# Where one block's 16-bit planes lie at the end of a mixer, and in which order three raw weight tiles are used in the first FFN group

## The chip, the cores and the metric

The kernel runs on one core of a Trainium2 chip. The metric is the device time of one execution in microseconds (us), taken as the median of several runs. TensorE (PE) multiplies matrices, ScalarE (ACT) and VectorE (DVE) work elementwise, GpSimd (POOL) has little to do here, and SyncE (SP) issues nearly all transfers (DMA). Each engine works through its own list of instructions strictly in order and waits for the others on semaphores. SP's list is a queue as well: an instruction that waits on SP holds back every load behind it.

## The reference

A decoder trunk of two layers over 256 tokens of width 2048, all in float32. Each layer adds a mixer and then a SwiGLU FFN to the residual stream `h`; a final RMS norm ends it.

```python
for layer in range(DEPTH):                     # DEPTH = 2
    xn = rms_norm(h, norm_mix[layer])
    if layer % 2 == 0:
        mix = swa_mlstm_mixer(xn, ...)         # ends in  @ w_out   (2048 x 2048)
    else:
        mix = forgetting_attention_mixer(xn, ...)   # ends in  @ w_out
    h = h + mix
    z = rms_norm(h, norm_ffn[layer])
    h = h + (silu(z @ w_gate) * (z @ w_up)) @ w_down    # hidden width 5632
return rms_norm(h, norm_final)
```

The change touches the stretch from the product with `w_out` to the first 512 hidden columns of the FFN (one "group"), once in each layer.

## The kernel before

**Products in three terms.** A float32 product is made of three matmuls of shortened operands: the operand is split into `hi` (a cast on ACT, L206 or L380) and `lo` (the difference on DVE, L207 or L381), and PE adds hi·hi (L557), hi·lo (L558) and lo·hi (L559; L244 to L246 in `gemm`). A load brings a raw chunk of 256 rows by 512 columns of weights (512 KB, L145).

**Mixed pairs.** In a group of the FFN (`pair_group`) gate and up are computed together over eight positions, `ORDER` (L36), each with 256 rows of both matrices. Five positions are plain: two chunks, each split and multiplied. Three, positions 1, 3 and 5, are mixed: the four 128-row blocks (two of gate, two of up) are combined so that seven products do the work of eight. Such a position has a **first stage**, one cast of three blocks (128x1536, L380) with its difference (L381), which fill a slot of `triples` (`hi0`/`lo0` or `hi1`/`lo1`, taken in turn), and a **second stage**, three subtractions in place on DVE (L645, L648, L649) and two more splits of 128x1024. On the other side of each mixed product stand sums of blocks of the activation (`sums_of`, L294 to L297, then a split into `sx`).

**Raw tiles of four blocks.** The raw weights of a mixed position land in a tile of four blocks taken from `quads`, which are used in turn (`quad()`, L113). There are three: two with the tag "quad" in the pool `fp`, and `own`, which lies on the sixth pair of weight planes of the pool `wp` (tag "hi"). The first five pairs are handed to the FFN as `stock`; out_proj's matmuls read the sixth until they end. Before the change `own` stands second in the list, so position 1 takes the first tile, position 3 takes `own`, and position 5 takes the last.

**The end of the mixer.** `out_proj` computes `m @ w_out` in four blocks of 512 columns, n = 0 to 3. `add_out` (L395) adds each to `h`; block n then has to be turned for the FFN, 512 columns at a time. `split_turned` copies it on ACT into two 16-bit planes (`flat`, L338), transposes these by DMA on SP's queue (L340, four transposes a block, into `turned`), and later a `join` on ACT puts the planes together again (two copies, L345) and splits the result into `xh` and `xl` with the gain (L386 on ACT, L387 on DVE). The joins of n = 0 and 1 run within out_proj. Those of n = 2 and 3 are handed on as `todo` and run at positions 3 and 5 of the first FFN group (`LATER`, L53), where the columns are first needed. `scrap(fp, n)` says where `flat` and `turned` lie: for even n in tag "c", for n = 3 in `sd0`/`sd1`, for n = 1 in a tile of tag "quad". The third tile of `quads` therefore has to wait until n = 1 is joined.

**What sets the order.** The program is written per position. The order on each engine is then made by a scheduler that simulates a timeline of the program, so a changed buffer can move instructions on every engine although no line of the loop is edited.

Of the kernel before, what the change touches and what calls it, by code (L numbers as in the profile page):

```python
# [7 lines left out]
F32 = mybir.dt.float32  # L8
BF16 = mybir.dt.bfloat16
F32R = mybir.dt.float32r  # L10
# [7 lines left out]
P = 128  # L18
# [5 lines left out]
NB = 512  # L24
CK = 2
# [29 lines left out]
QUADS = 2  # L55
# [13 lines left out]
def mixed_of(order):  # L69
    return [p for w, p in order if w]  # L70
# [5 lines left out]
def trunk(  # L76
# [27 lines left out]
    stock, triples, quads = [], [], []  # L104

    def slot():
        if not stock:
            both = wp.tile([P, 2, CK, NB], F32R, tag="hi", name="hi")
            return [both[:, a, :, :] for a in range(2)]
        stock.append(stock.pop(0))  # L110
        return stock[-1]
# [255 lines left out]
    def scrap(fp, n):  # L367
        if n % 2 == 0:
            box = fp.tile([P, 4, NB], F32, tag="c", name="box", bufs=1)
            halves = box[:, 0:2, :], box[:, 2:4, :]  # L370
        elif n == 3:
            halves = [fp.tile([P, 3, NB], F32, tag=f"sd{i}", name="box", bufs=1)[:, 0:CK, :] for i in range(2)]
        else:
            box = fp.tile([P, 2 * CK, NB], F32, tag="quad", name="box", bufs=QUADS)
            halves = box[:, 0:2, :], box[:, 2:4, :]
        flat, turned = (a.rearrange("p a n -> p (a n)") for a in halves)
        return flat, turned.bitcast(U16).rearrange("p (b k t q) -> p b k t q", b=2, t=NT, q=P)

# [147 lines left out]
    def spare_halves():  # L526
        return [
            tuple(
                m[:, 8 + 4 * a : 12 + 4 * a, :].rearrange("p k s -> p (k s)").rearrange("p (c n) -> p c n", c=2)
                for m in (mh, ml)  # L530
            )
            for a in range(2)
        ]

    def out_proj(w, idx, key, extra):
        last, rest = KT - 4, []
        for n0 in (0, 2):
            accs = [new_acc() for _ in range(2)]
            for i in range(2):
                gemm(accs[i], m_of, w, (n0 + i) * NB, NB, 0, last, KT, step=6 * i)  # L540
            for i in range(2):
                gemm(accs[i], m_of, w, (n0 + i) * NB, NB, last, KT, KT, step=6)
                add_out(accs[i], n0 + i)
                (later if n0 == 0 else rest).append(
                    (LATER[n0 + i], split_turned(idx, n0 + i, *scrap(extra[3], n0 + i), extra))
                )
                square_sum(key, n0 + i)
        return rest
# [119 lines left out]
    def ffn(layer, fp, sx, x4, sd, key, todo, idx_next=None, key_next=None, finish=None):  # L668
# [8 lines left out]
        for g0, g1 in zip(PARTS, PARTS[1:]):  # L677
# [81 lines left out]
            def close(acc, n):  # L759
                if not end:  # L760
                    add_out(acc, n)
                elif idx_next is None:
                    finish(acc, n, gf)
                else:
                    add_out(acc, n)
                    if n < 1:
                        todo.append((LATER_DOWN[n], split_turned(idx_next, n, *scrap(fp, n))))
                    else:
                        split_scaled(idx_next, n)
                    square_sum(key_next, n)  # L770
# [25 lines left out]
    def close_layer(layer, w_out, idx, key, **rest):  # L796
        with tc.tile_pool(name=f"fp{layer}", bufs=2) as fp:
            junk_of[:] = fp, "tmp", 2
            nx = len(mixed_of(ORDER))
            nd = max(len(mixed_of(o)) for o in DOWN.values())  # L800
            sx = [fp.tile([P, nx, 4, P], F32R, name=f"sx{i}", bufs=1) for i in range(2)]
            x4 = fp.tile([P, 2, P], F32R, name="x4", bufs=1)
            todo = out_proj(w_out, idx, key, (*sx, x4, fp))
            sd = [fp.tile([P, nd, 4, P], F32R, tag=f"sd{i}", name=f"sd{i}", bufs=1) for i in range(2)]
            triples.extend([fp.tile([P, 3, NB], F32R, name=f"{a}{i}", bufs=1) for a in ("hi", "lo")] for i in range(2))
            stock.extend([slot() for _ in range(5)])
            own = wp.tile([P, 2, CK, NB], F32R, tag="hi", name="raw").rearrange("p a k n -> p (a k) n").bitcast(F32)
            quads.extend(fp.tile([P, 2 * CK, NB], F32, tag="quad", name="raw", bufs=QUADS) for _ in range(QUADS))
            quads.insert(1, own)
            ffn(layer, fp, sx, x4, sd, key, todo, **rest)  # L810
            stock.clear()
            triples.clear()
            quads.clear()
# [3 lines left out]
    hi, lo = slot()  # L817
# [17 lines left out]
    with tc.tile_pool(name="ev", bufs=1) as ev:  # L835
# [225 lines left out]
        with tc.tile_pool(name="mp", bufs=1) as mp:  # L1061
# [8 lines left out]
            halves = spare_halves()  # L1070
# [115 lines left out]
    for n in range(4):  # L1186
        nc.gpsimd.dma_start(h[:, :, n * NB : (n + 1) * NB], xv[:, :, n * NB : (n + 1) * NB])

    close_layer(0, w_out_even[0], 2, "f0", idx_next=1, key_next="m1")


    r1 = rstd("m1")
    wi1 = w_in_odd[0]
    with tc.tile_pool(name="od", bufs=1) as od:
# [70 lines left out]
        halves = spare_halves()  # L1265
# [67 lines left out]
    def finish(acc, n, gf):  # L1333
        for t in range(NT):
# [31 lines left out]
            nc.scalar.dma_start(ov[:, t, NB : 2 * NB], b1)  # L1366

    close_layer(1, w_out_odd[0], 3, "f1", finish=finish)


# [47 lines left out]
```

## Time and profile before

| | |
|---|---|
| runs | 2088.95, 2090.94, 2092.37 us; median 2090.94 us |
| profiled execution, its own time | 2090.14 us |
| its span in the trace | 2088.4 us (1.74 us lie around it) |
| busy | PE 2071.4 us (99%), DVE 1806.3 us (86%), ACT 1367.1 us (65%), POOL 44.0 us (2%) |
| in layer 0: end of out_proj, start of the FFN | about 323.3 us from the span's start |
| in layer 1: the same | about 1386 us |

A row of a timeline gives the start of an instruction (or of several alike in a row, "x2"), its duration, engine, line, operation, output and input; in brackets stand the idle time before it on its engine and what ended that. A row of windows gives a stretch of time, for each engine the busy time and the number of instructions, then the granted clock of PE (1.00 is full), the share of the time the DMA engines were busy, and GB/s. PE's matmuls are pipelined: one of 512 columns is listed with some 0.39 us, and starts follow each other every 0.227 us where nothing is missing. So for PE the number of matmuls in a stretch says more than its busy time.

### The profile page before, as it was taken

The page shows a single profiled execution, that of the slowest core. Times are in us where ns is not written, and L with a number is a line of the kernel's source. Part 1 is how long each engine was busy: PE and PEld are TensorE (multiplying, and loading weights), DVE is VectorE, ACT ScalarE, POOL GpSimd, SP SyncE. Part 2 cuts the span into 40 slices and gives each one's busy share as a digit, 9 for nine tenths or more (in the row PEclk, how much of TensorE's full clock was granted, in tenths as well). Part 3 has the DMA queues.
Part 4 walks back from the last instruction along what each step waited for, and adds up shares of the span by engine and source line. Part 5 has one row for each costly group of instructions (what it writes and reads, how often), then busy time and mean ns, then how long its engine had stood idle before and what let it go on. Part 6 is the DMA issues. An engine that isn't in the chain of part 4 may idle for free.

```text
span 2088.4 us, 26470 instructions
## 1 busy us (share of the span) xinstructions
PE 2071.4 (99%) x9473; PEld 1714.7 (82%) x9473; DVE 1806.3 (86%) x2169; ACT 1367.1 (65%) x1649; POOL 44.0 (2%) x69
## 2 busy tenths in 40 slices
PE   9999999999999999999999999999999999999998
PEld 7878887888888888888888888877888888888887
DVE  6788768989999989998899688679989999999984
ACT  6777677665577646667677676587655667556763
POOL 1010000000000000000000001000000000000000
PEclk9999999999999999999999999999999999999999
DMA  8566577765677666665676776585756766666754
GB/s 292 174 207 194 188 242 215 222 200 198 205 221 224 210 194 224 217 209 184 203 202 218 225 200 185 155 269 188 250 188 196 233 196 217 226 205 200 235 158 159
DMA packets 309572, 434.84 MB, mean 208 GB/s; under 512 B 106413, under 2 KB 114625, under 8 KB 309313
## 3 DMA queue, kind: packets, MB, share of 16 engines
q1 hardware_dynamic: 307088, 426.27, 65.1%
q0 software_dynamic: 1632, 5.80, 0.9%
q8 instruction: 74, 1.21, 0.2%
q10 hardware_dynamic: 720, 1.09, 0.2%
q14 instruction: 58, 0.47, 0.1%
HBM read 408.68 MB, written 2.12 MB: 197 GB/s over the span
## 4 chain that ended last, share of the span: by engine, by line
PE 89%; ACT 4%; DVE 3%; DMA 2%; issue 2%; SPq 0%; POOL 0%; POOLq 0%; ACTq 0%; DVEq 0%
PE acc L558 20%; PE acc L559 20%; PE acc L557 20%; PE prod L558 5%; PE prod L557 5%; PE prod L559 5%; PE acc L245 4%; PE acc L244 4%; PE acc L246 4%; DVE hi L207 1%; ACT box L345 1%; PE p L411 1%; ACT hi L206 1%; ACT hi L380 1%; DMA raw<-in_w_gate_dram 1%
## 5 line engine op out<-in xcount | busy, mean ns | idle before, releaser
L206 ACT CAST hi<-raw 128x1024 fp32r<-128x1024 f32 (+3 forms) x561 | 567.1, 1023 | 366.5 <-PE acc L559 179.4
L207 DVE TENSOR_TENSOR hi<-raw,hi 128x1024 fp32r<-128x1024 f32 (+3 forms) x561 | 657.9, 1186 | 137.2 <-ACT hi L206 134.7
L559 PE MATMUL acc<-hi,xl 128*128 128x512 f32 x1320 | 511.9, 389 | 0.0
L557 PE MATMUL acc<-hi,xh 128*128 128x512 f32 x1320 | 495.9, 390 | 0.8 <-ACT xh L386 0.6
L380 ACT CAST hi<-raw 128x1024 fp32r<-128x1024 f32 (+2 forms) x299 | 344.9, 1168 | 225.8 <-PE acc L559 192.7
L558 PE MATMUL acc<-hi,xh 128*128 128x512 f32 x1254 | 488.0, 390 | 0.2 <-DVE hi L207 0.2
L557 PEld LDWEIGHTS acc<-hi,xh 128*128 128x128 f32 x1320 | 247.6, 188 | 53.5 <-ACT xh L386 1.8
L559 PEld LDWEIGHTS acc<-hi,xl 128*128 128x128 f32 x1320 | 248.0, 188 | 51.5
L558 PEld LDWEIGHTS acc<-hi,xh 128*128 128x128 f32 x1254 | 235.4, 188 | 50.0 <-DVE hi L207 1.0
L381 DVE TENSOR_TENSOR hi<-raw,hi 128x1024 fp32r<-128x1024 f32 (+1 forms) x204 | 240.2, 1180 | 11.1 <-ACT hi L380 10.4
L381 DVE TENSOR_TENSOR lo<-raw,hi 128x1536 fp32r<-128x1536 f32 x95 | 166.6, 1754 | 43.6 <-ACT hi L380 40.0
L559 PE MATMUL acc<-hi,ml 128*128 128x512 f32 x466 | 181.0, 389 | 0.0
L557 PE MATMUL acc<-hi,mh 128*128 128x512 f32 x466 | 173.3, 389 | 0.0
L558 PE MATMUL acc<-hi,mh 128*128 128x512 f32 x437 | 170.3, 390 | 0.4 <-DVE hi L207 0.4
L245 PE MATMUL acc<-hi,mh 128*128 128x512 f32 (+1 forms) x322 | 126.3, 392 | 0.0
L244 PE MATMUL acc<-hi,mh 128*128 128x512 f32 (+1 forms) x322 | 125.8, 391 | 0.0
L246 PE MATMUL acc<-hi,ml 128*128 128x512 f32 (+1 forms) x322 | 123.7, 391 | 0.0
L645 DVE TENSOR_TENSOR raw<-raw 128x1024 f32<-128x1024 f32 x95 | 115.5, 1217 | 0.4
L557 PEld LDWEIGHTS acc<-hi,mh 128*128 128x128 f32 x466 | 87.5, 188 | 18.6 <-ACT hi L206 0.4
L559 PEld LDWEIGHTS acc<-hi,ml 128*128 128x128 f32 x466 | 87.5, 188 | 18.1
L245 PE MATMUL acc<-hi,xh 128*128 128x512 f32 (+3 forms) x288 | 99.8, 347 | 0.2 <-DVE hi L207 0.2
L246 PE MATMUL acc<-hi,xl 128*128 128x512 f32 (+3 forms) x288 | 99.1, 345 | 0.0
(364 smaller groups left out, 3073.9 us busy)
## 6 DMA issues: line engine op xcount, KB each, us to landing
raw<-in_w_gate_dram SPq DMA_DIRECT2D x176, 512.0 KB, 4.3
raw<-in_w_up_dram SPq DMA_DIRECT2D x176, 512.0 KB, 4.8
raw<-in_w_down_dram SPq DMA_DIRECT2D x176, 512.0 KB, 4.8
raw<-in_w_in_odd_dram SPq DMA_DIRECT2D x88, 512.0 KB, 5.2
raw<-in_w_in_even_dram SPq DMA_DIRECT2D x51, 512.0 KB, 5.0
raw<-in_w_out_even_dram SPq DMA_DIRECT2D x32, 512.0 KB, 5.3
raw<-in_w_out_odd_dram SPq DMA_DIRECT2D x32, 512.0 KB, 4.7
hr<-in_w_in_even_dram SPq DMA_DIRECT2D x12, 512.0 KB, 4.4
```

Source lines behind the costliest of these rows:

```text
L206: latest[0] = nc.scalar.copy(hi[:, k, 0:n], raw[:, k, 0:n])
L207: nc.vector.tensor_tensor(out=lo[:, k, 0:n], in0=raw[:, k, 0:n], in1=hi[:, k, 0:n].bitcast(F32), op=ALU.subtract)
L244: nc.tensor.matmul(o, ah[:, ts], hi, start=(k == 0), stop=False)
L245: nc.tensor.matmul(o, ah[:, ts], lo, start=False, stop=False)
L246: nc.tensor.matmul(o, al[:, ts], hi, start=False, stop=(k == k_all - 1 and cs.stop == n))
L345: nc.scalar.copy(ju[:, :, b], turned[:, b, :, :, :].rearrange("p k t q -> p (k t q)"))
L380: cast = nc.scalar.copy(dst_h, src)
L381: nc.vector.tensor_tensor(out=dst_l, in0=src, in1=dst_h.bitcast(F32), op=ALU.subtract)
L557: nc.tensor.matmul(o, ah, hi, start=start, stop=False)
L558: nc.tensor.matmul(o, ah, lo, start=False, stop=False)
L559: nc.tensor.matmul(o, al, hi, start=False, stop=stop)
L645: nc.vector.tensor_tensor(out=raw[:, 1:4:2, :], in0=raw[:, 3:4, :].broadcast_to([P, 2, NB]), in1=raw[:, 1:3, :], op=ALU.subtract)
```

## The change

The planes of block n = 1 get another place, the second slot of `triples` (`hi1` for `flat`, `lo1` for `turned`, two of the three blocks of each). The tiles of `triples` carry explicit tags for that. And `own` moves from second to last in the list of `quads`. No line of arithmetic and no size is edited.

```diff
@@ scrap(fp, n): where the planes of h's block n lie
         elif n == 3:
             halves = [fp.tile([P, 3, NB], F32, tag=f"sd{i}", name="box", bufs=1)[:, 0:CK, :] for i in range(2)]
         else:
-            box = fp.tile([P, 2 * CK, NB], F32, tag="quad", name="box", bufs=QUADS)
-            halves = box[:, 0:2, :], box[:, 2:4, :]
+            halves = [fp.tile([P, 3, NB], F32, tag=f"{a}1", name="box", bufs=1)[:, 0:CK, :] for a in ("hi", "lo")]
@@ close_layer
-            triples.extend([fp.tile([P, 3, NB], F32R, name=f"{a}{i}", bufs=1) for a in ("hi", "lo")] for i in range(2))
+            triples.extend([fp.tile([P, 3, NB], F32R, tag=f"{a}{i}", name=f"{a}{i}", bufs=1) for a in ("hi", "lo")] for i in range(2))
             stock.extend([slot() for _ in range(5)])
             own = wp.tile([P, 2, CK, NB], F32R, tag="hi", name="raw").rearrange("p a k n -> p (a k) n").bitcast(F32)
             quads.extend(fp.tile([P, 2 * CK, NB], F32, tag="quad", name="raw", bufs=QUADS) for _ in range(QUADS))
-            quads.insert(1, own)
+            quads.append(own)
```

Behind line 374 the changed kernel's line numbers are one lower (L380 becomes L379). The names carry numbers. Before, the tiles of positions 1, 3 and 5 are raw_2993, raw_2992 (`own`) and raw_2994; in the changed kernel they are raw_2994, raw_2995 and raw_2993 (`own`).

The first place is SP's queue in layer 0's out_proj, around the transposes of n = 0 (box_2579) and n = 1 (box_2647, now box_2647 and box_2648). Before:

```order
L145 DMA raw_2713<-in_w_out_even_dram 128x2x512
L145 DMA raw_2730<-in_w_out_even_dram 128x2x512
L145 DMA raw_2747<-in_w_out_even_dram 128x2x512
L145 DMA raw_2764<-in_w_out_even_dram 128x2x512
L145 DMA raw_2781<-in_w_out_even_dram 128x2x512
L340 DMA_TRANSPOSE box_2579<-box_2579 128x4x128 x4
L340 DMA_TRANSPOSE box_2647<-box_2647 128x4x128 x4
L145 DMA raw_2798<-in_w_out_even_dram 128x2x512
```

Now:

```order
L145 DMA raw_2994<-in_w_gate_dram 128x2x512
L145 DMA raw_2714<-in_w_out_even_dram 128x2x512
L145 DMA raw_2994<-in_w_up_dram 128x2x512
L145 DMA raw_2731<-in_w_out_even_dram 128x2x512
L145 DMA raw_2995<-in_w_gate_dram 128x2x512
L145 DMA raw_2995<-in_w_up_dram 128x2x512
L145 DMA raw_2748<-in_w_out_even_dram 128x2x512
L145 DMA raw_2765<-in_w_out_even_dram 128x2x512
L340 DMA_TRANSPOSE box_2579<-box_2579 128x4x128 x4
L340 DMA_TRANSPOSE box_2648<-box_2647 128x4x128 x4
L145 DMA raw_2782<-in_w_out_even_dram 128x2x512
```

All four loads of positions 1 and 3 have moved ahead of the eight transposes of n = 0 and 1, and one `w_out` load (raw_2781 before, raw_2782 now) has moved behind them.

The second place is the same queue at the start of layer 0's FFN, where the planes of n = 2 (box_2922, now box_2923) and n = 3 (box_2969 and box_2970, now box_2970 and box_2971) are transposed. Before:

```order
L145 DMA raw_2994<-in_w_up_dram 128x2x512
L145 DMA raw_3004<-in_w_gate_dram 128x2x512
L145 DMA raw_3020<-in_w_up_dram 128x2x512
L145 DMA raw_3072<-in_w_gate_dram 128x2x512
L145 DMA raw_3088<-in_w_up_dram 128x2x512
L145 DMA raw_3156<-in_w_gate_dram 128x2x512
L145 DMA raw_3172<-in_w_up_dram 128x2x512
L145 DMA raw_2993<-in_w_gate_dram 128x2x512
L340 DMA_TRANSPOSE box_2922<-box_2922 128x4x128 x4
L145 DMA raw_2992<-in_w_gate_dram 128x2x512
L340 DMA_TRANSPOSE box_2970<-box_2969 128x4x128 x4
L145 DMA raw_2992<-in_w_up_dram 128x2x512
```

Now:

```order
L145 DMA raw_3157<-in_w_gate_dram 128x2x512
L145 DMA raw_3173<-in_w_up_dram 128x2x512
L340 DMA_TRANSPOSE box_2923<-box_2923 128x4x128 x4
L340 DMA_TRANSPOSE box_2971<-box_2970 128x4x128 x4
L145 DMA raw_2993<-in_w_gate_dram 128x2x512
L145 DMA raw_2993<-in_w_up_dram 128x2x512
L145 DMA raw_3243<-in_w_gate_dram 128x2x512
```

The loads of `own` stood between and behind the two groups of transposes and fed position 3; now they stand behind both and feed position 5.

The third place is ACT at the same time. Before:

```order
L206 CAST hi_2987<-raw_3088 128x1024
L380 CAST hi0_2983<-raw_2994 128x1536
L345 COPY box_2969<-box_2970 128x1024 x2
L206 CAST hi_2990<-raw_3156 128x1024
L380 CAST hi1_2985<-raw_2992 128x1536
L345 COPY box_2922<-box_2922 128x1024 x2
L386 ACTIVATE xh_58<-box_2969,gT_93 128x256 x4
L206 CAST hi_2991<-raw_3172 128x1024
L386 ACTIVATE xh_58<-box_2922,gT_93 128x256 x4
```

Now:

```order
L206 CAST hi_2988<-raw_3089 128x1024
L345 COPY box_2923<-box_2923 128x1024 x2
L379 CAST hi_2989<-raw_2995 128x1024
L385 ACTIVATE xh_58<-box_2923,gT_93 128x256 x4
L326 ACTIVATE full_3119<-box_2923,gT_93 128x256 x2
L379 CAST hi_2990<-raw_2995 128x1024
L206 CAST hi_2991<-raw_3157 128x1024
L379 CAST hi0_2984<-raw_2993 128x1536
L345 COPY box_2970<-box_2971 128x1024 x2
L206 CAST hi_2992<-raw_3173 128x1024
```

Before, the cast of position 3's three blocks (into hi1_2985) stood behind the join of n = 3. Now that cast (into hi1_2986) has left this stretch and stands in out_proj, ahead of the last two `w_out` casts; the join of n = 2 comes first, position 3's second-stage casts come next, and the join of n = 3 is behind the three-block cast of position 5. Layer 1 shows the same moves at its mixer's end, with two differences: the four early loads stand there in one run ahead of the last `w_out` load before the eight transposes, and of `own`'s two loads one stands between the transposes of n = 2 and n = 3 and one behind (before, both stood between). On POOL nothing has moved.

## The prediction

> **What bounds the kernel now.** I read the page first: the span, the busy shares and the chain that ended last.
>
> ```profile
> span 2088.4 us, 26470 instructions
> PE 2071.4 (99%) x9473; PEld 1714.7 (82%) x9473; DVE 1806.3 (86%) x2169; ACT 1367.1 (65%) x1649; POOL 44.0 (2%) x69
> PE 89%; ACT 4%; DVE 3%; DMA 2%; issue 2%; SPq 0%; POOL 0%; POOLq 0%; ACTq 0%; DVEq 0%
> ```
>
> PE bounds it nearly everywhere. A change that edits no arithmetic can win only where PE has holes or runs at a lower clock, so next I took windows around the place of the change, in layer 0 and in layer 1 (columns: busy time and count of PE, PEld, DVE, ACT, POOL; granted clock; DMA share; GB/s).
>
> ```profile
> 270.00:300.00 30.00, 30.00 (x135) 24.82 (x134) 17.19 (x24) 21.35 (x32) 0.00 (x0) 1.00 0.69 207
> 325.00:340.00 15.00, 14.14 (x63) 11.38 (x61) 7.97 (x10) 9.74 (x13) 0.69 (x1) 1.00 0.96 210
> 340.00:362.00 22.00, 18.37 (x70) 13.56 (x71) 21.82 (x29) 19.20 (x27) 0.00 (x0) 0.92 0.53 177
> 362.00:400.00 38.00, 38.00 (x170) 31.45 (x169) 37.38 (x45) 27.51 (x29) 0.00 (x0) 1.00 0.67 211
> 1335.00:1360.00 25.00, 25.00 (x112) 20.70 (x111) 13.12 (x19) 17.80 (x26) 0.00 (x0) 1.00 0.52 143
> 1403.00:1422.00 19.00, 16.99 (x68) 11.80 (x67) 18.41 (x30) 17.54 (x26) 0.00 (x0) 1.00 0.43 137
> ```
>
> The counts tell what the busy shares hide. From 362 to 400 us PE works through 170 matmuls in 38 us, 0.2235 us each. At that pace the 70 matmuls of 340 to 362 need 15.65 us and took 22: **6.35 us** are lost. The 63 of 325 to 340 need 14.08 of 15: **0.9 us** more. In layer 1 the 68 matmuls of 1403 to 1422 need 15.2 us of 19: **3.8 us** lost. Out_proj (270 to 300, 1335 to 1360) loses nothing: 135 matmuls in 30 us are 0.222 each.
>
> What ended the holes stands in PE's own timeline, the first seven rows in layer 0, the last two in layer 1:
>
> ```profile
> 338.75 0.39 PE L559 MATMUL acc<-hi,xl 128*128 128x512 f32 x1
> 341.17 0.50 PE L557 MATMUL prod<-hi,xh 128*128 128x512 f32 x1 [2.03 <-ACT hi L380]
> 342.96 0.80 PE L558 MATMUL prod<-lo,xh 128*128 128x512 f32 x1 [0.83 <-DVE lo L381]
> 343.98 0.63 PE L558 MATMUL acc<-lo,xh 128*128 128x512 f32 x1
> 344.41 0.63 PE L559 MATMUL acc<-hi,xl 128*128 128x512 f32 x1
> 346.53 0.50 PE L557 MATMUL acc<-hi,xh 128*128 128x512 f32 x1 [0.64 <-ACT xh L386]
> 355.40 0.50 PE L558 MATMUL prod<-hi,sx 128*128 128x512 f32 x1 [0.99 <-DVE hi L381]
> 1406.66 0.50 PE L557 MATMUL prod<-hi,xh 128*128 128x512 f32 x1 [0.69 <-ACT xh L386]
> 1410.94 0.72 PE L557 MATMUL prod<-hi,sx 128*128 128x512 f32 x2 [0.66 <-ACT hi L380]
> ```
>
> In layer 0 position 3 (the first `prod` row behind 338.75) waits for its three-block cast and then for the difference: 2.03 + 0.83 us. Behind that the starts are 0.43 us apart instead of 0.227: the clock was halved. In layer 1 the first wait is for the join's split (`xh` L386), not for the position's cast, and the holes stay below 0.7 us each. The cause in layer 0 is read on ACT and SP:
>
> ```profile
> 336.28 2.56 ACT L345 COPY box<-box 128x1024 uint16<-128x1024 uint16 x2 [3.99 <-DMA box<-box]
> 339.64 1.47 ACT L380 CAST hi<-raw 128x1536 fp32r<-128x1536 f32 x1
> 323.47 5.61 SPq L340 DMA_TRANSPOSE box<-box  x4
> 329.18 0.53 SPq L145 DMA_DIRECT2D raw<-in_w_gate_dram  x1
> 329.80 5.14 SPq L340 DMA_TRANSPOSE box<-box  x4
> 335.00 0.58 SPq L145 DMA_DIRECT2D raw<-in_w_up_dram  x1
> 306.53 0.37 SPq L145 DMA_DIRECT2D raw<-in_w_gate_dram  x1
> ```
>
> `own`, position 3's raw tile, is loaded at 329.18 and 335.00, around the second group of transposes. ACT stands 3.99 us idle for the transposes of n = 3, which the order put first, and reaches position 3's cast at 339.64, 0.66 us after PE could have begun (338.98, a spacing behind 338.75) and 1.5 us too late with its 1.47 us. Position 5's raw tile was loaded already at 306.53, long before it is needed.
>
> **The change part by part.**
>
> *Position 3's first stage leaves the hole.* Its four blocks are now loaded ahead of out_proj's transposes, and its cast stands ahead of out_proj's last two `w_out` casts, near 305 us. It needs 1.47 us on ACT (row above) and on DVE what position 1's took before:
>
> ```profile
> 307.43 1.76 DVE L381 TENSOR_TENSOR lo<-raw,hi 128x1536 fp32r<-128x1536 f32 x1
> 310.24 1.22 DVE L645 TENSOR_TENSOR raw<-raw 128x1024 f32<-128x1024 f32 x1
> 314.25 0.69 DVE L648 TENSOR_TENSOR raw<-raw 128x512 f32<-128x512 f32 x1
> ```
>
> With L649, of the same shape as L648, that is 4.36 us of DVE. Position 1's same stage, which stood at these rows, moves forward to about 273 to 282, where DVE works 17.19 of 30 us and ACT 21.35; so both are hidden by PE's matmuls. Without that cover a stage would cost up to 1.47 + 4.36 = 5.8 us a layer.
>
> *Position 5 takes `own`.* Its loads now wait behind both groups of transposes on SP, which from 323.47 need 5.61 + 5.14 us and end near 334.2. Gate and up, half a microsecond each to issue, land some 5 us later, by 340. Position 3 is 7 products of three matmuls, position 4 is 24 matmuls; so PE, which starts position 3 at 338.98, reaches position 5 after 45 x 0.2235 = 10.1 us, at 349.0. Cast 1.47 and difference 1.76 fit with some 6 us to spare. In layer 1 `own`'s gate is issued ahead of n = 3's transposes, so no later.
>
> *The joins.* ACT no longer idles for n = 3. Before, ACT got n = 3's planes 1.34 us after SP was done with them (336.28 less 329.80 + 5.14). So n = 2's, done at 329.08, are there by 330.4; the join takes 2.56 us, and position 3's second-stage casts behind it end by about 338.5, when PE gets there. So the holes of 2.03, 0.83 and 0.64 us go, and with them the half clock. What is late next is DVE:
>
> ```profile
> 350.00 1.22 DVE L381 TENSOR_TENSOR hi<-raw,hi 128x1024 fp32r<-128x1024 f32 x1
> ```
>
> It has 21.82 us of work in the 22 us of 340 to 362. Position 3's first stage (4.36 us) leaves that stretch, position 5's enters it; ahead of 340, where DVE was busy for 7.97 us of 15, go the work on n = 2's join and position 3's two second-stage differences (2 x 1.22 us). But PE comes 7 us earlier too. Walking these durations through the new order I find margins of 0 to 1 us between 353 and 365.
>
> The most that can be won is 6.35 + 0.9 + 3.8 = **11.1 us**. What stays is unknown. From below: nothing. From above: the loss of layer 1, **3.8 us a layer**, since there position 3's cast did not set the first wait and PE still lost that. I take 1.2 us a layer, nearer to zero, because the walk finds every operand ready, if barely, and ACT has 3.99 us of idle time to give: **+2.4 us**.
>
> [...]
>
> ```profile
> 342.00:343.00 1.00, 0.17 (x2) 0.04 (x1) 0.96 (x2) 1.00 (x2) 0.00 (x0) 0.92 0.98 240
> 343.00:344.00 1.00, 1.00 (x3) 0.81 (x4) 1.00 (x1) 1.00 (x3) 0.00 (x0) 0.50 0.97 375
> ```
>
> Idle pieces of 2.03 and 0.83 us, with three matmuls between them, sufficed. So a remaining hole under 0.7 us, as in layer 1 where the clock stayed 1.00, costs its own length, and one of 2 us may cost its length again. [...]
>
> *Out_proj.* Two margins shrink there.
>
> ```profile
> 268.83 0.37 SPq L145 DMA_DIRECT2D raw<-in_w_out_even_dram  x1
> 276.62 1.29 DVE L395 TENSOR_TENSOR h<-acc,h 128x512 f32<-128x512 f32 x2 [2.45 <-PE acc L246]
> 279.82 0.39 PE L244 MATMUL acc<-hi,mh 128*128 128x512 f32 x1
> 280.48 10.37 SPq L340 DMA_TRANSPOSE box<-box  x8
> 296.27 1.05 ACT L206 CAST hi<-raw 128x1024 fp32r<-128x1024 f32 x1 [1.89 <-DMA raw<-in_w_out_even_dram]
> 297.35 1.23 DVE L207 TENSOR_TENSOR hi<-raw,hi 128x1024 fp32r<-128x1024 f32 x1 [2.87 <-ACT hi L206]
> 299.54 0.39 PE L244 MATMUL acc<-hi,mh 128*128 128x512 f32 x1
> DMA to landing us min/median/max: 3.5/5.3/7.9
> ```
>
> First, position 1's difference (1.76) and first subtraction (1.22) now stand ahead of `add_out` of n = 0 on DVE. Its up half follows the `w_out` load of 268.83 on SP, near 269.3; landed 5.3 us later, cast 1.47, differenced and subtracted, that ends near 279.0. Each of add_out's two halves takes 0.65 us, so the first bank is free at 279.7, and the products of n = 2 start into it at 279.82: hidden, by 0.1 us. Second, one `w_out` load moves behind the eight transposes, which end at 290.85. Issued there, landed 5.3 us later, cast (1.05) and split (1.23), it is ready at 298.5; its first matmul is at 299.54, so 1.0 us of cover. Below: nothing; above, with the longest landing of 7.9 us: 2.5 us in the one place or 1.6 in the other, and the half clock behind it. I take **+0.4 us** in all.
>
> Sum: -11.1 + 2.4 + 0.4 = **-8.3 us**. The profiled execution took 2090.14 us (a span of 2088.4 and 1.74 around it); it becomes 2081.8. That execution lies 0.80 us below the median of the runs shown, so the forecast is **2082.6 us** beside 2090.94.
>
> **Rivals.**
>
> 1. *The joins bind anyway.* Each layer keeps 3.8 us, as layer 1 has now: DVE's 21.82 of 22 us speak for it, ACT's idle 3.99 us and the early cast against. Gain 7.25 - 3.8 = 3.45 in layer 0, none in layer 1: **2087.5 us**.
>
> 2. *Out_proj pays (slower).* The four early loads, 2 MB, stand among the `w_out` chunks, and position 1's stage stands ahead of `add_out`. If the up half takes the 7.9 us, the first bank is free at 282.3: PE waits 2.5 us at 279.82, the clock halves, 2 us more. The planes of n = 0 and 1, their transposes and the chunk behind them come late by as much, which uses up the second margin of 1.0 us and costs up to 1.5 us and 1 of clock. Some 7 us a layer: 2082.6 - 0.4 + 14 = **2096 us**. It decides from a landing above 5.4 us in the first place and a delay above 1 us on SP in the second. For it: a DMA share of 0.69 in 270 to 300, so the early loads share the engines. Against: in layer 1 the same stretch has a share of 0.52, and what is loaded early need not be loaded between 291 and 325, so the queue catches up.
>
> 3. *The wait moves to position 5.* `own` is loaded last; if SP reaches it 7 us later than I count, position 5 stalls some 2 us: **2085 us**. Only a transposes' delay of that size would do it, and none shows.
>
> 4. *The whole 11.1 us is won*, if nothing is left over: 2079.8 us.
>
> **How the numbers follow.** Forecast 0.57, rival 1 0.18, rival 2 0.13, rival 3 0.04, rival 4 0.08. A measurement of this kernel tells about 0.2% from no change, 4.2 us: below 2086.8 is faster, above 2095.1 slower. Forecast, rivals 3 and 4 and a fifth of rival 1 are faster: 0.73. The rest of rival 1 and a third of rival 2 are no change: 0.18. Two thirds of rival 2 are slower: 0.09. The range goes from 2079.0, a little below rival 4, to 2089.5, beyond rival 1, which leaves out rival 2 and some edges, about 0.16. The forecast's own range is 2080.5 to 2086, from the bounds of the two unknown costs.
>
> **What would show it.** In the changed profile the stretch that was 325 to 362 should hold some 30 more matmuls at the old times, no granted clock of 0.50, ACT without the 3.99 us wait, and no `prod` row that waits for L379's three-block cast at position 3; the first FFN group should begin at 323.3 as before, give or take 0.5. In layer 1 the holes of 0.69 and 0.66 us should shrink. Rival 1 would show as waits on `xh` L385 or on DVE's differences near 340 to 360 that add up to 3.8 us; rival 2 as PE idle and a low clock between 279 and 305 or 1340 and 1375, with `add_out` or a `w_out` chunk named; rival 3 as a wait for the three-block cast near 349. I am wrong if out_proj starts the FFN later than 325 us, or if layer 1 loses as much as before.

## The result, and the profile after

The changed kernel takes 2084.06 us (median of 7 runs, 2083.45 to 2085.02) against 2091.95 us before (7 runs, 2088.95 to 2093.99): ratio 0.9964, 95% interval 0.9954 to 0.9973. That is 7.9 us, between 5.6 and 9.6. Forecast were a gain of 8.3 us and a time of 2082.6.

The page of the changed kernel: span, busy shares, and the chain by engine.

```profile
span 2082.6 us, 26464 instructions
PE 2068.5 (99%) x9473; PEld 1714.7 (82%) x9473; DVE 1805.5 (87%) x2169; ACT 1367.6 (66%) x1649; POOL 42.8 (2%) x69
PE 85%; DVE 6%; ACT 3%; DMA 3%; issue 2%; SPq 0%; POOL 0%; POOLq 0%; ACTq 0%; DVEq 0%
```

PE is busy 2.9 us less and the span is 5.8 us shorter; the work of ACT and DVE is what it was. The windows, in the same stretches as before (the FFN starts at 324.8 us now in layer 0, 323.3 before, and 4.0 us earlier than before in layer 1):

```profile
270.00:300.00 30.00, 28.27 (x125) 23.07 (x124) 17.74 (x25) 19.70 (x30) 0.00 (x0) 1.00 0.70 217
325.00:340.00 15.00, 15.00 (x68) 12.43 (x67) 9.04 (x17) 15.00 (x25) 0.69 (x1) 1.00 0.50 114
340.00:362.00 22.00, 21.33 (x92) 16.70 (x91) 19.84 (x27) 18.90 (x24) 0.00 (x0) 1.00 0.77 273
1335.00:1360.00 25.00, 25.00 (x112) 20.72 (x111) 17.00 (x24) 19.85 (x29) 0.00 (x0) 1.00 0.63 194
1403.00:1422.00 19.00, 18.43 (x80) 14.31 (x78) 18.60 (x25) 16.74 (x24) 0.00 (x0) 1.00 0.65 209
```

From 325 to 362 us PE now gets 160 matmuls done where it had been 133 (27 more, where some 30 were forecast), at a clock of 1.00; from 1403 to 1422 it is 80 for 68. And out_proj, which lost nothing before, has 125 where it had 135. The holes that are left, in PE's own timeline:

```profile
281.08 0.50 PE L244 MATMUL acc<-hi,mh 128*128 128x512 f32 x1 [1.73 <-DVE h L394]
348.58 0.50 PE L557 MATMUL acc<-hi,xh 128*128 128x512 f32 x1 [0.30 <-DVE hi L207]
356.52 0.50 PE L557 MATMUL acc<-hi,xh 128*128 128x512 f32 x1 [0.37 <-DVE hi L207]
1413.28 0.50 PE L556 MATMUL prod<-hi,sx 128*128 128x512 f32 x1 [0.21 <-ACT hi L379]
1416.65 0.50 PE L557 MATMUL acc<-hi,xh 128*128 128x512 f32 x1 [0.35 <-DVE hi L207]
1427.81 0.50 PE L557 MATMUL acc<-hi,xh 128*128 128x512 f32 x1 [0.67 <-DVE hi L207]
```

No row waits for position 3's cast any more. The largest hole is new, and it is in out_proj: 1.73 us for `add_out` (L394).

To compare kernels whose holes lie in different places, the table counts for each profile where PE's matmul starts are more than 0.26 us apart, and adds up what is over 0.227. The stretches are cut by the number of the matmul, so that each holds the same work in all kernels. (Of the span's 5.8 us, 0.6 were won ahead of out_proj, where the two kernels are the same: a difference between two executions.)

| lost by PE, us | out_proj, layer 0 | FFN start, layer 0 (77 us) | from there to layer 1's out_proj | FFN start, layer 1 (64 us) | behind it |
|---|---|---|---|---|---|
| before | 0.35 | 7.17 | 1.97 | 4.13 | 0.89 |
| changed | 2.36 | 1.84 | 1.95 | 2.31 | 0.87 |
| changed, two more profiles | 2.43; 1.63 | 1.17; 0.71 | 1.96; 1.96 | 2.01; 2.63 | 0.87; 0.88 |

In layer 1's out_proj it is 0.94 for all of them. So 11.3 us of holes became 4.2 (3.2 and 3.3 in the other profiles), and out_proj pays 2.0 (2.1, 1.3): by the sum of all columns 5.2 us are won in this profile, 6.1 and 6.7 in the others.

### The profile page after: what moved, and what is told of

Its sections match the earlier page's. It is cut to its first block, busy times and chain, and to the rows that moved or that the text cites. A ratio compares the mean times of both kernels' runs of the same rounds, so it can differ in the third digit from the quotient of the medians.

```text
span 2082.6 us, 26464 instructions
## 1 busy us (share of the span) xinstructions
PE 2068.5 (99%) x9473; PEld 1714.7 (82%) x9473; DVE 1805.5 (87%) x2169; ACT 1367.6 (66%) x1649; POOL 42.8 (2%) x69
## 4 chain that ended last, share of the span: by engine, by line
PE 85%; DVE 6%; ACT 3%; DMA 3%; issue 2%; SPq 0%; POOL 0%; POOLq 0%; ACTq 0%; DVEq 0%
PE acc L557 20%; PE acc L558 20%; PE acc L556 19%; PE prod L556 5%; PE prod L558 5%; PE prod L557 5%; PE acc L244 3%; PE acc L245 3%; PE acc L246 3%; DVE hi L207 2%; DMA raw<-in_w_up_dram 1%; ACT box L345 1%; DMA raw<-in_w_gate_dram 1%; ACT hi L206 1%; PE p L410 1%
## 5 line engine op out<-in xcount | busy, mean ns | idle before, releaser
L206 ACT CAST hi<-raw 128x1024 fp32r<-128x1024 f32 (+3 forms) x561 | 567.6, 1023 | 355.2 <-PE acc L558 188.5
L207 DVE TENSOR_TENSOR hi<-raw,hi 128x1024 fp32r<-128x1024 f32 (+3 forms) x561 | 659.2, 1188 | 129.7 <-ACT hi L206 127.5
L379 ACT CAST hi<-raw 128x1024 fp32r<-128x1024 f32 (+2 forms) x299 | 345.6, 1168 | 229.2 <-PE acc L558 178.4
L380 DVE TENSOR_TENSOR hi<-raw,hi 128x1024 fp32r<-128x1024 f32 (+1 forms) x204 | 241.0, 1183 | 15.9 <-ACT hi L379 15.3
L380 DVE TENSOR_TENSOR lo<-raw,hi 128x1536 fp32r<-128x1536 f32 x95 | 166.7, 1755 | 47.0 <-ACT hi L379 46.8
```

The source lines that it names most:

```text
L206: latest[0] = nc.scalar.copy(hi[:, k, 0:n], raw[:, k, 0:n])
L207: nc.vector.tensor_tensor(out=lo[:, k, 0:n], in0=raw[:, k, 0:n], in1=hi[:, k, 0:n].bitcast(F32), op=ALU.subtract)
L379: cast = nc.scalar.copy(dst_h, src)
L380: nc.vector.tensor_tensor(out=dst_l, in0=src, in1=dst_h.bitcast(F32), op=ALU.subtract)
```

## The experiments

Two theories about the gain. **A**: position 3 no longer takes `own`, so it no longer waits for a load that can't start before out_proj's end. **B**: the new place of the planes frees a raw tile early. And two about the loss in out_proj. **C**: position 1's first stage stands ahead of `add_out` on DVE and waits for its load. **D**: the burst of early loads makes the `w_out` chunks themselves late.

**The changed kernel again**, as the mark on the chip of the next three.

> The changed kernel again, as the mark for the others on the same chip. By its profile PE gains 5.24 us between matmul 1323 (260 us) and the end: 6.68 us at layer 0's first FFN group and 3.81 us at layer 1's, less 2.07 us in layer 0's out_proj and some 3.2 us in holes that open later in both groups. All theories: 5 to 9 us below the kernel before.

2084.1 us against 2091.25, ratio 0.9966 (0.9953 to 0.9978): 7.2 us.

**Only the order of the tiles.**

```diff
  (the kernel before)
-            quads.insert(1, own)
+            quads.append(own)
```

> Only the order of the raw tiles is changed (own last); the planes of n = 1 stay in the tile with the tag quad. Theory A (the gain is that position 3 no longer takes own, which can only be loaded when out_proj is over): the whole gain at both FFN groups, and no loss in out_proj, since the loads of position 1 and 3 stay where they were before; 1 to 3 us below the changed kernel, so 7 to 10 us below before. Theory B (the gain comes from where the planes lie, which frees a raw tile early): within 2 us of before.

2085.96 us, ratio 0.9974 (0.9964 to 0.9984): 5.3 us faster than before, 1.9 slower than the changed kernel. PE loses 0.35 us in out_proj as before, and only 1.23 and 0.56 at the FFN starts: the whole gain there, and more than the changed kernel's. So the place of `own` in the list makes the gain, as A has it; the time missed what was expected with A (7 to 10 us below before). But behind the FFN starts it loses 4.20 and 3.06 us where the others lose 2 and 0.9. Over all columns of the table that makes 9.4 us, about what the changed kernel loses (9.3, 8.4 and 7.8). The largest holes of that kind in PE's timeline:

```profile
410.56 0.50 PE L557 MATMUL acc<-hi,xh 128*128 128x512 f32 x1 [0.32 <-DVE c L579]
468.81 0.50 PE L557 MATMUL acc<-hi,mh 128*128 128x512 f32 x1 [0.77 <-ACT mh L380]
471.88 0.51 PE L557 MATMUL acc<-hi,mh 128*128 128x512 f32 x1 [0.46 <-ACT hi L380]
```

They lie some 85 and 145 us behind the FFN's start, in parts of it that the edit does not touch, and where the instructions now stand in another order; the last experiment shows one of them.

**Only the place of the planes.**

```diff
  (the changed kernel)
-            quads.append(own)
+            quads.insert(1, own)
```

> Only the place of the planes is changed; own stays second in the list. Theory A: position 3 still waits for own, whose two loads now stand between the transposes of n = 2 and n = 3, so holes of 3 to 6 us stay at layer 0's FFN start and some 3 us at layer 1's, and out_proj still loses 2 us: between 2 us faster and 3 us slower than before. Theory B: as the changed kernel, 5 to 9 us faster.

2090.18 us, ratio 0.9995 (0.9986 to 1.0004): not to be told from no change, so B falls. The holes at layer 1's FFN start are those of before, one by one; two of them, in PE's timeline:

```profile
1405.62 0.50 PE L556 MATMUL prod<-hi,xh 128*128 128x512 f32 x1 [0.70 <-ACT xh L385]
1409.90 0.73 PE L556 MATMUL prod<-hi,sx 128*128 128x512 f32 x2 [0.67 <-ACT hi L379]
```

Before they were 0.69 and 0.66 us. PE loses 4.13 us there, as before. In layer 0 it loses 4.16 (before 7.17), and out_proj loses 2.20 (before 0.35). So the place of the planes by itself wins 3.0 us at one FFN start, pays 1.85 in out_proj, and brings the loss there that the changed kernel has.

The 3.0 us show the path. `own` is still position 3's tile, but its two loads now follow each other ahead of n = 3's transposes (329.60 and 330.17 us), ACT no longer waits for those transposes first, and the cast, at 335.15, is in time. PE waits for the joins instead, as in layer 1, and the joins stand on ACT behind that cast, which waits for `own`'s load. Layer 1 before, then layer 0 here:

```profile
1397.71 1.48 ACT L380 CAST hi<-raw 128x1536 fp32r<-128x1536 f32 x1 [2.31 <-DMA raw<-in_w_up_dram]
1399.10 5.01 ACT L345 COPY box<-box 128x1024 uint16<-128x1024 uint16 x4
```

```profile
335.15 1.48 ACT L379 CAST hi<-raw 128x1536 fp32r<-128x1536 f32 x1 [1.93 <-DMA raw<-in_w_up_dram]
336.54 5.00 ACT L345 COPY box<-box 128x1024 uint16<-128x1024 uint16 x4
```

**`add_out` first.**

```diff
  (the changed kernel; added holds add_out of n = 1, t = 1)
-                latest[0] = split_plain(hg, lg, raw[:, 0:3, :])
+                if added:
+                    with tc.issue_after(added.pop().ins):
+                        latest[0] = split_plain(hg, lg, raw[:, 0:3, :])
+                else:
+                    latest[0] = split_plain(hg, lg, raw[:, 0:3, :])
```

> The changed kernel, with position 1's first stage of the first FFN group queued on ACT and DVE behind add_out of n = 1. Theory C (the 1.73 us hole at 281 us is the bank that waits for add_out, which stands on DVE behind the difference of a raw tile whose load landed 7 us after its issue): no hole in out_proj, PE 2.07 us earlier at the end of out_proj in layer 0; 1 to 3 us below the changed kernel. Rival D (the six loads issued within 3 us make the w_out chunks themselves late, and add_out is only the first to show it): a hole of over 1 us at a w_out chunk's cast (L206) or difference (L207) between 279 and 300 us, and the time of the changed kernel.

2082.45 us, ratio 0.9956 (0.9944 to 0.9969), 1.65 us below the changed kernel, though the runs of the two overlap. Out_proj loses 0.35 us as before, while the early loads are issued where the changed kernel issues them, and no `w_out` chunk is late. So C holds and D falls. At layer 0's FFN start the new order costs more (3.32 us, with one hole of 1.52 us for an L206 that stands behind n = 3's join on ACT), and less in layer 1 (0.52).

**The planes in the first slot.**

```diff
  (the changed kernel)
-            halves = [fp.tile([P, 3, NB], F32, tag=f"{a}1", name="box", bufs=1)[:, 0:CK, :] for a in ("hi", "lo")]
+            halves = [fp.tile([P, 3, NB], F32, tag=f"{a}0", name="box", bufs=1)[:, 0:CK, :] for a in ("hi", "lo")]
```

> The changed kernel with the planes of n = 1 in the first slot of triples (hi0, lo0) in place of the second. Position 1's first stage needs that slot and so cannot start before n = 1 is joined, near 305 us; position 3's takes the second slot, and on DVE stands behind add_out of n = 1. Theory C (the out_proj hole is position 1's stage ahead of add_out on DVE): no hole at 281 us in layer 0, so some 2 us below the changed kernel, unless the scheduler's order of the FFN groups changes too: the holes there as in the changed kernel, 1 to 2.5 us a layer. Rival D (the burst of early loads is the cause): the loads stand as in the changed kernel, so the hole stays and the time is that of the changed kernel.

2080.8 us, ratio 0.995 (0.9938 to 0.9963): 10.0 us below before, and the fastest kernel of this study. The same windows:

```profile
270.00:300.00 30.00, 30.00 (x134) 24.83 (x133) 19.96 (x26) 20.79 (x30) 0.00 (x0) 1.00 0.92 256
340.00:362.00 22.00, 21.02 (x91) 16.36 (x90) 19.95 (x26) 18.38 (x23) 0.00 (x0) 1.00 0.78 269
```

Out_proj is whole again, with the early loads and a DMA share of 0.92, which is more than in the changed kernel (0.70): once more C and not D. Position 1 has to wait for n = 1's join, and so its first stage can't stand in front of `add_out`. PE loses 1.69 us at layer 0's FFN start, and in layer 1 nothing at all. With the changed kernel beside it on one chip:

> The changed kernel once more, as the mark for the three beside it: 6 to 9 us below before, with a hole of 1.7 us at 281 us, one of 0.5 us at 348 and one of 0.5 us at 356.

> The kernel with the planes of n = 1 in the first slot of triples once more: 2 to 4 us below the changed kernel on the same chip, if the difference seen between two chips is the kernel's.

2083.03 us for the changed kernel, ratio 0.9962 (0.9948 to 0.9975), and 2080.54 us for the planes in the first slot, 0.9948 (0.9936 to 0.9961), against 2091.24. The difference, 2.5 us, is 0.12%; the two intervals overlap, but in all of their runs on this chip the ranges don't (2082.41 to 2084.68, 2080.0 to 2080.7). The holes of the changed kernel were not where they were expected: 1.00 us at 280.33, and, by the starts, none of over 0.25 us between 340 and 362. So these holes come and go between executions of one kernel. The one in out_proj goes with the landing of position 1's up half: 7.4, 7.5 and 6.8 us from its issue to its cast in the three profiles, and holes of 1.73, 1.81 and 1.00 us.

**`own` first.**

```diff
  (the changed kernel)
-            quads.append(own)
+            quads.insert(0, own)
```

> The changed kernel with own first in the list, so that position 1 waits for it. Theory A (own can only be loaded when out_proj is over, so its place in the list decides): its loads are issued at about 324.5 us, land near 330, and PE reaches position 1 at 330; cast 1.47 and difference 1.76 us and the three subtractions follow, so holes of 3 to 7 us and a halved clock in each layer, 8 to 18 us slower than the changed kernel. If its place hardly matters: within 3 us of the changed kernel.

2088.89 us, ratio 0.9991 (0.9982 to 1.0): some 5 us slower than the changed kernel, and not the 8 to 18 that were expected. PE loses 5.08 us at layer 0's FFN start and 4.17 in layer 1, while out_proj loses nothing. But this is not the wait that A expects. SP's, ACT's and PE's rows in layer 0, where the FFN starts at 322.75:

```profile
316.74 1.17 SPq L145 DMA_DIRECT2D raw<-in_w_up_dram  x2
322.92 1.48 ACT L379 CAST hi<-raw 128x1536 fp32r<-128x1536 f32 x1 [0.93 <-DMA raw<-in_w_up_dram]
327.77 2.57 ACT L345 COPY box<-box 128x1024 uint16<-128x1024 uint16 x2 [2.75 <-DMA box<-box]
332.71 1.03 ACT L206 CAST hi<-raw 128x1024 fp32r<-128x1024 f32 x1
333.79 0.73 PE L556 MATMUL acc<-hi,xh 128*128 128x512 f32 x2 [2.72 <-ACT hi L206]
```

`own`'s up half is one of the two loads at 316.74, some 5 us ahead of out_proj's end: in this kernel `own` lies on a pair of planes that out_proj gives up 39 matmuls sooner than in the changed kernel. No other weights are loaded from there to 336.48, and position 1's last subtraction on DVE ends at 329.37, so its cast is the one at 322.92, and that is in time. PE's 2.72 us are for the cast of a plain position, which stands on ACT behind the join of n = 2, and that waited 2.75 us for its transposes; position 1's second-stage casts stand there too. So this run shows again that the place of `own` sets the order on ACT, and what that costs; it does not show a late load, and it is no test of A.

**What is left at the FFN's start.** Theory **E**: DVE has no room. Rival **F**: an order or a latency. The four small sums of the joins of n = 2 and 3 went to GpSimd, in the kernel with only `quads.append(own)`:

```diff
-        nc.vector.tensor_tensor(out=s[:, 0, :], in0=full[:, 0, 1, :], in1=full[:, 1, 1, :], op=ALU.add)
+        eng.tensor_tensor(out=s[:, 0, :], in0=full[:, 0, 1, :], in1=full[:, 1, 1, :], op=ALU.add)
...
-                    sums_of(pool, rooms(xh), rooms(xl), copies, x4=x4)
+                    sums_of(pool, rooms(xh), rooms(xl), copies, x4=x4, eng=nc.gpsimd)
...
```

> The kernel with own last and the planes in the quad tile, with the four small sums (128x128, 0.28 us each on DVE) of the joins of n = 2 and 3 on GpSimd. Theory E (what is left at the FFN's start is DVE, which has no slack between 340 and 365 us): 2.3 us less DVE work in each layer's first group; the holes there and in the next group (1.23 and 2.25 us in layer 0, 0.56 and 2.2 in layer 1 in that kernel) shrink, 1 to 4 us in all. Rival F (an order on ACT or the latency of a chain is the cause): no gain; and if GpSimd needs over 1 us for each sum, the split of the sums comes late and PE waits for sx, 1 to 4 us slower.

2082.69 us, ratio 0.9962 (0.9948 to 0.9975): 8.1 us below before on its chip, where the same kernel with the sums on DVE was 5.3 below on another. But the gain is not where E wants it: the FFN starts lose more (2.42 and 1.69 us for 1.23 and 0.56), and the later holes (4.20 and 3.06) are down to 2.17 and 0.87. As the order changed everywhere, this run can't tell E from F. The kernel with the planes in the first slot can: in layer 1 it loses nothing, in both of its profiles, with all the sums on DVE. So DVE's amount of work alone does not force holes there. What leaves them in the changed kernel is not shown.

**The one that stays in layer 0.** Theory **G**: ACT waits for `own`'s load, and position 4's last cast is queued behind. In the changed kernel, ACT:

```profile
342.41 1.48 ACT L379 CAST hi<-raw 128x1536 fp32r<-128x1536 f32 x1 [1.89 <-DMA raw<-in_w_up_dram]
343.79 2.57 ACT L345 COPY box<-box 128x1024 uint16<-128x1024 uint16 x2
346.22 1.05 ACT L206 CAST hi<-raw 128x1024 fp32r<-128x1024 f32 x1
```

`own`'s up half is issued at 337.34 and there by 342.4. Its cast itself is early enough, but the L206 at 346.22 is of position 4, and its difference on DVE is what PE waits for at 348.58. The edit queues the three-block cast of position 5 behind it, in the kernel with the planes in the first slot and in the changed kernel:

```diff
-                latest[0] = split_plain(hg, lg, raw[:, 0:3, :])
+                if todo and pos == 5:
+                    with tc.issue_after(latest[0].ins):
+                        latest[0] = split_plain(hg, lg, raw[:, 0:3, :])
+                else:
+                    latest[0] = split_plain(hg, lg, raw[:, 0:3, :])
```

> The planes in the first slot, and in the first FFN group position 5's three-block cast queued on ACT behind the cast of position 4's last chunk. Theory G (the hole near 346 us in layer 0 is ACT, which stands for own's load, landed 5 us after its issue behind eight transposes, with position 4's cast queued behind it): that hole of 1.0 us goes, and PE reaches the next group 0.5 to 1.5 us earlier in layer 0; nothing in layer 1, where no hole was left. Rival E (DVE has no room there): the hole stays within 0.3 us or opens again before 365 us.

> The changed kernel with the same one queueing. Theory G: the hole at 348 us (0.46 us and a slow start behind it) goes, 0.3 to 1.0 us in layer 0, while the hole of 1.73 us at 281 us stays. Rival E: unchanged within 0.3 us.

With the edit the hole is in neither profile. But without it the gap between the two starts is 0.46 us too long in one profile of the changed kernel and not at all in the other two; with the planes in the first slot it is 0.77 in one and 0.32 in the other. So G fits, and one profile each does not show it. In the changed kernel the whole FFN start of layer 0 loses 0.00 us with the edit, for 0.71 to 1.84, so DVE has room for a group without any hole; the hole of out_proj stays, with 1.53 us. In the other kernel new holes open at 352.18 and 355.89, and 1.30 us stay. Yet both kernels became slower: 2084.3 us (0.9966, 0.9954 to 0.9979) and 2088.51 us (0.9986, 0.9977 to 0.9995). Between layer 0's FFN start and layer 1's out_proj they lose 5.43 and 6.10 us where it had been 2.18 and 1.95, and behind layer 1's FFN start 2.0 for 0.9. One of those holes, in PE's timeline, with what stands on ACT there:

```profile
467.53 0.50 PE L556 MATMUL acc<-hi,mh 128*128 128x512 f32 x1 [0.70 <-ACT mh L379]
```

```profile
464.14 2.86 ACT L379 CAST hi<-raw 128x1536 fp32r<-128x1536 f32 x2 [0.51 <-PE prod L558]
466.90 1.06 ACT L379 CAST mh<-pf 128x512 fp32r<-128x512 f32 x2
```

With the planes in the first slot and without the edit, ACT has it the other way round:

```profile
463.33 1.08 ACT L379 CAST mh<-pf 128x512 fp32r<-128x512 f32 x2 [2.13 <-PE pf L714]
464.29 1.49 ACT L379 CAST hi<-raw 128x1536 fp32r<-128x1536 f32 x1
```

The scheduler, after an edit some 120 us earlier, put two three-block casts ahead of the split into `mh` (the `hi` part of the hidden activation, for the product with `w_down`) that PE needs at once. "Only the order of the tiles" has holes of the same size at the same places (468.81 and 471.88), also with two such casts ahead of `mh` on ACT.

## Why the prediction was right, point by point

- **The bound, and what could be won.** The holes were measured at 7.25 + 3.8 us by counts, and are 7.17 + 4.13 by the gaps. "Only the order" shows that they go with `own`'s place, in both layers, and "Only the place" shows the path: 3.0 us of layer 0 went with position 3's late cast and the half clock behind it (granted from 340 to 362 us: 0.92 before, 1.00 in that run), and the other 4.16 were, like layer 1's 4.13, mainly the joins that stand on ACT behind that cast. The prediction named the late load in layer 0; of layer 1 it said that position 3's cast did not set the first wait, and missed that the join it saw there stood behind it.
- **Position 3's first stage hidden in out_proj.** It is, and ACT's wait of 3.99 us is gone (windows 325 to 340: ACT 15.00 of 15). Both forecast, and shown.
- **What stays, forecast at 2.4 us with an upper bound of 7.6.** It is 4.2, 3.2 and 3.3 us in three profiles: a third to three quarters more than forecast. The term that was too small is the 1.2 us taken for each layer: layer 0 measured 1.8, 1.2 and 0.7, layer 1 2.3, 2.0 and 2.6. The walk through the new order was made with layer 0's rows alone. In it, "some 6 us to spare" for position 5 counted when its own cast is needed, and not what is queued behind that cast on ACT while it waits for the load; that fits one hole of one profile (G). For the rest, most of it in layer 1 and named by L207, the cause was not found.
- **Out_proj, forecast at 0.4 us.** It is 2.0, 2.1 and 1.3. The place and the mechanism were those written down (add_out behind position 1's difference); the size failed with the landing. The FFN begins at 324.8, 325.1 and 324.0 us in the three profiles, where 323.3 was forecast and 325 named as the sign of being wrong. The up half, the third of six loads that SP issues between 266.7 and 270.6 us, took 7.4 us and not the 5.3 of the median, which was that of the `w_out` loads:

```profile
268.48 0.46 SPq L145 DMA_DIRECT2D raw<-in_w_up_dram  x1
275.89 1.48 ACT L379 CAST hi<-raw 128x1536 fp32r<-128x1536 f32 x1 [3.61 <-DMA raw<-in_w_up_dram]
277.40 1.76 DVE L380 TENSOR_TENSOR lo<-raw,hi 128x1536 fp32r<-128x1536 f32 x1 [3.87 <-ACT hi L379]
279.19 1.23 DVE L644 TENSOR_TENSOR raw<-raw 128x1024 f32<-128x1024 f32 x1
280.34 1.28 DVE L394 TENSOR_TENSOR h<-acc,h 128x512 f32<-128x512 f32 x2
```

  This is the first half of rival 2. Its second half didn't come: the transposes began at 282.74 us, 2.3 us later than before, but PE was 1.4 us later there too, so the `w_out` chunk behind them (cast at 298.19) was still in time. Layer 1 lost nothing in out_proj.
- **That the gain came so close, 7.9 us for 8.3, is partly luck.** By the terms of the profiles the sum is -11.3 + 4.2 + 2.0 = -5.1 us where -8.3 was forecast; with all columns of the table it is 5.2, and two more profiles give 6.1 and 6.7. The medians of three sets of runs give 7.9, 7.2 and 8.2. So the terms, as they stand in the profiles, explain some 5 to 7 of about 7.7 us. Both errors, what stays and out_proj, make the gain smaller, and the medians hide them: the profiled execution of before, 2090.14 us, lies 0.7 to 1.8 us below the medians of its runs. What fills the gap no profile shows.
- **The clock.** No window of the FFN starts shows 0.50 any more, as forecast. I feared that a hole of 2 us costs its length again; the new one of 1.73 us in out_proj did not, the clock stays 1.00 through it (rows in the last section). Rival 2 has 3 us a layer, 6 in all, for a half clock in out_proj: my estimate, and no run shows it there.
- **Rivals.** The joins alone don't bind (rival 1): with `own` last and no other edit the FFN starts lose 1.23 and 0.56 us. Position 5 doesn't stall for its own cast (rival 3).

## What to carry to other kernels

When a buffer becomes free late, ask which use of it comes first, and what is queued behind that use: putting the late buffer last in the rotation won nearly all that was lost at the FFN starts. Moving the planes won 3.0 us there by itself and paid 1.85 elsewhere. When prefetches become possible earlier, the work on them lands in the engines' queues ahead of older work (here DVE stood 3.87 us for a tile loaded early, with `add_out` behind it): count what stands behind a waiting instruction on its engine, and ask whether a median landing time fits loads that are issued in a burst (6.8 to 7.5 us here, beside a median of 5.3; that the burst made the difference was not tested). And where a scheduler makes the order, look at PE's holes over the whole program for each edit: holes of 2 us a layer came and went some 120 us from the line that was edited, which is as much as the edits were worth.

## What the runs showed of the hardware that was not expected

The granted clock fell to 0.50 around some holes and stayed 1.00 around another of nearly their length. The rows are stretches of 3.41 us, as long as the 0.50 lasted in the kernel before, each followed by the next: before, around the holes of 2.03 and 0.83 us; with `own` first, around a hole of 2.72 us in layer 0 and one of 1.80 us in layer 1; and the changed kernel, where the first row holds its whole hole of 1.73 us.

```profile
339.43:342.84 3.41, 0.97 (x3) 0.49 (x3) 2.92 (x2) 3.41 (x4) 0.00 (x0) 1.00 1.04 366
342.85:346.25 3.40, 2.93 (x6) 1.83 (x6) 3.37 (x7) 3.40 (x7) 0.00 (x0) 0.50 0.36 134
346.27:349.67 3.40, 3.13 (x12) 2.28 (x13) 3.40 (x8) 3.40 (x8) 0.00 (x0) 1.00 0.26 51
```

```profile
331.60:335.01 3.41, 1.00 (x3) 0.56 (x4) 1.56 (x4) 3.41 (x7) 0.69 (x1) 1.00 0.38 77
335.02:338.42 3.40, 3.40 (x9) 2.66 (x9) 3.40 (x9) 3.40 (x8) 0.00 (x0) 0.50 0.56 92
1393.15:1396.55 3.40, 1.38 (x6) 0.52 (x4) 1.38 (x3) 3.40 (x6) 0.70 (x1) 1.00 0.38 77
1396.56:1399.96 3.40, 3.40 (x8) 2.66 (x9) 3.40 (x9) 3.40 (x8) 0.00 (x0) 0.50 0.52 95
```

```profile
279.31:282.72 3.41, 1.68 (x8) 1.36 (x8) 3.41 (x5) 1.66 (x4) 0.00 (x0) 1.00 0.35 132
282.73:286.13 3.40, 3.40 (x17) 2.79 (x16) 3.40 (x5) 2.51 (x4) 0.00 (x0) 1.00 0.38 77
```

PE was busy for 0.97, 1.00 and 1.38 us of the stretch ahead of each 0.50, and for 1.68 us of the one that holds the hole of 1.73 us, where the clock stayed 1.00. What decides between them these four cases do not show.

GpSimd needed 0.45 to 1.44 us each for the sums of 128x128 that were moved to it, which take DVE 0.28 in the kernel before; two of them, in layer 0:

```profile
337.93 0.45 POOL L297 TENSOR_TENSOR s<-full 128x128 f32<-128x128 f32 x1
338.34 1.44 POOL L296 TENSOR_TENSOR s<-s,full 128x128 f32<-128x128 f32 x1
```
